# Shift and scale weights by single feature tiles, gates by way of DRAM rows, three output tiles begun early

## The chip, the cores and the metric

The kernel runs on one core of a Trainium2 chip. The metric is the device time of one execution in microseconds (us), median of several runs. The engines named below are TensorE (PE; its weight loads are listed as PEld), VectorE (DVE), ScalarE (ACT), GpSimd (POOL) and SyncE (SP, which here only issues DMAs). DMAs are issued from SP, ACT and POOL.

## The reference, cut to what matters

One inference step of a two-layer trunk over 512 latent and 128 context tokens, model width 1024. Layer 0 is gated attention (16 query heads, 4 key/value heads of 64), layer 1 a gated linear recurrence of 8 heads in both directions. Each layer is modulated by shift, scale and gate vectors that come from two conditioning vectors:

```python
def _adaln(cond, w, b):
    mod = jax.nn.silu(cond.astype(jnp.float32)) @ w.astype(jnp.float32) + b.astype(jnp.float32)
    return jnp.split(mod.astype(cond.dtype), 3, axis=-1)

for i in range(DEPTH):
    sh_p, sc_p, g_p = _adaln(c_ctx, ada_w[i], ada_b[i])
    sh_s, sc_s, g_s = _adaln(c, ada_w[i], ada_b[i])
    hp = xp * (1.0 + sc_p) + sh_p
    hs = xs * (1.0 + sc_s) + sh_s
    ...
    xp = _layer_norm(DEEPNORM_ALPHA * xp + g_p * out_p, ln_gain[i], ln_bias[i])
    xs = _layer_norm(DEEPNORM_ALPHA * xs + g_s * out_s, ln_gain[i], ln_bias[i])
```

The shift and the scale of layer 0 are needed before the first projection; a gate vector is needed only at the end of its layer, where it multiplies the rows of the output projection before the residual sum and the layer norm.

## The kernel before

Tokens stand in five tiles of 128 (four latent, one context). Feature-major operands have eight feature tiles (`ft`) of 128. Every product of weights and activations is three matmuls (high by high, high by low, low by high): a float32 weight piece of 128 x 1024 (512 KB, tile `raw`) is split by an ACT cast (line 218) and a DVE subtraction (line 219) into a high and a low part. `order` lists all pieces in the sequence in which SP loads them; `pump` issues the next loads while no more than a set number are ahead (8 at the start, then 2). Loads passed to `pin` keep their program order on SP. The program as written is not the order of the instructions: a planner places each engine's stream by program order and by when it reckons that inputs and buffers are ready, and for everything up to line 1037 it does so with a simulated timeline.

**The lead** (lines 415 to 483). Four rounds `c4`, each for two feature tiles. `flip` transposes x on TensorE. `ada_mms` multiplies SiLU(cond) by a piece of `ada_w` holding 256 columns and half of the depth, so a column chunk takes two pieces, and shift and scale take two chunks, four pieces, a round. `ada_row` copies the result out of PSUM, `ada_out` turns it into columns with two small matmuls (line 275) and adds the bias into `shsc` (line 279). `modulate` applies shift and scale on DVE (line 441) and splits into `hhi` (ACT, line 443) and `hlo` (DVE, line 444). `kv_mms` (lines 460 to 462) then accumulates keys and values of all five token tiles over the feature tiles. The rotary table and the two gains are loaded from POOL's queue at the start (lines 419, 421), and POOL makes four tables of them (line 424).

**The other modulation chunks** run beside attention. `q_gen` projects the queries of the next group as side work and calls `next(fill)` at fixed places, where `fill` is `ada_gen` over some chunks: the gate of layer 0 beside group 1, the shift, scale and gate of layer 1 later. For a gate chunk `ada_out` fills the column tile `gcol`, and `spread` (lines 285 to 292) broadcasts the columns over partitions: four matmuls against the identity (eight records, line 291, `gateps`) and a DVE copy into `gate` (line 292). For layer 0 that comes in `ada_gen`; for layer 1 in the tail.

**The second half.** `proj_gen(h)` projects head h of the recurrence (`vgps`, then three parts i = 0 to 2 in `rps`, lines 1108 to 1110), `evac` evaluates the gates of part i. `gla_gen(h)` runs the recurrence of a head beside the projection of the next head: seven levels (`lv`, line 1238 or 1244, with DVE updates of `A` at lines 1247 and 1252 and an ACT copy `kc` at line 1216), then `kp` (1278), `sp` (1284) with state updates on DVE (1287, 1290), `op` (1301 to 1304), a normalisation (1309 to 1315), `oT` (1320) and the split result `ghi`, `glo` (1321, 1322). `Residual` prepares the residual rows in DRAM on POOL. PSUM holds four tiles of two banks in this half.

**The tail** (lines 1368 to 1424). The last head's recurrence has no projection beside it. `weave` runs it with `tail_gen` at a ratio of 2.2 side steps per step: `tail_gen` splits the eight pieces of `rec_w_out` in the order `OUT1`, spreads the gate of layer 1, and accumulates k = 0 to 6 of the output tiles 0 and 1 (`out_mms`, lines 993 to 995, `outp`; k is the head). After the last head, k = 7 of these two and all of tiles 2, 3 and 4 follow, and `Norm` does gate, residual and layer norm of each tile on DVE (`half`: lines 1013 to 1015; `finish`: 1020 to 1030), one POOL power (line 189), and two output DMAs (line 1031).

Of the kernel before, what the change touches and what calls it, by code (L numbers as in the profile page):

```python
# [18 lines left out]
P = 128  # L19
# [112 lines left out]
def hybrid_step(ctx: ExitStack, tc: tile.TileContext, a: dict, o: dict):  # L132
# [49 lines left out]
    gcol1 = const.tile([P, 4, 2, 2], F32, name="gcol1")  # L182
# [12 lines left out]
    def pump():  # L195
        while order:
            start = order[0] in FIRST
            if len(ahead) >= (RAW_START if start else RAW_AHEAD):
                break
            src = order.popleft()  # L200
            if src[0] == "x":
                c = slice(src[1] * CW, (src[1] + 1) * CW)
                pin(nc.sync.dma_start(xt[:, :TS, c], a["xs"][:, c].rearrange("(t p) d -> p t d", p=P)))
                pin(nc.sync.dma_start(xt[:, TS, c], a["xp"][:, c]))
                continue
            raw = (raw0 if start else rawp).tile([P, 1024], F32, tag="raw", name="raw")
            (pass_on if src[0][:3] == "rec" else pin)(nc.sync.dma_start(raw, piece(src)))
            ahead.append((src, raw))
# [55 lines left out]

    def ada_row(ps):
        row = rowp.tile([P, CW], F32, tag="row", name="row")
        nc.vector.tensor_copy(row, ps[:, :CW])
        return row

    def ada_out(layer, c, row):  # L270
# [7 lines left out]
        if part < 2:  # L278
            nc.vector.tensor_tensor(shsc[layer][:, part, 2 * c4:2 * c4 + 2, :], src, bias, ALU.add)
            return None  # L280
        gcol = gcol1[:, c4] if layer else tiny.tile([P, 2, 2], F32, tag="gc", name="gcol")[:]
        nc.vector.tensor_tensor(gcol, src, bias, ALU.add)
        return None if layer else lambda: spread(layer, c4, gcol)

    def spread(layer, c4, gcol):

        ps = bank1("gateps")
        for s in range(2):
            for j in range(2):
                col = bass.AP(gcol.tensor, gcol.offset + 2 * j + s, [list(gcol.ap[0]), [0, P]])  # L290
                nc.tensor.matmul(ps[:, (2 * s + j) * P:(2 * s + j + 1) * P], col, ident, start=True, stop=True)
        nc.vector.tensor_copy(gate[layer][:, :, c4 * CW:(c4 + 1) * CW], ps[:].rearrange("p (a b) -> p a b", a=2))

    def ada_gen(chunks):
        todo, last = None, None
        for l, c in chunks:
# [3 lines left out]
            if last:  # L300
                last()
            last = todo and ada_out(*todo)
            yield
            todo = (l, c, ada_row(ps))
        if last:
            last()
        if todo:
            last = ada_out(*todo)
            yield
            if last:  # L310
                last()
                yield
# [21 lines left out]
    x1d = [dram.tile([P, D], F32, name=f"x1d{tt}") for tt in range(TT)]  # L334
    x1a = [dram.tile([P, D], F32, name=f"x1a{tt}") for tt in range(TT)]
# [27 lines left out]
    order.extend(("rec_w_out", nh, i) for nh, i in OUT1)  # L363
# [51 lines left out]
    with pool("xin", 1) as xin:  # L415
# [3 lines left out]
        nc.gpsimd.dma_start(rope, a["rope"])  # L419
        for g, nm in ((qg, "q_gain"), (kg, "k_gain")):  # L420
            nc.gpsimd.dma_start(g, a[nm].to_broadcast((P, HD)))
        nc.gpsimd.tensor_scalar(qg, qg, 1.0 / math.sqrt(HD), 1.0, ALU.mult, ALU.mult)
        for t, r, g in ((cosq, 0, qg), (sinq, 1, qg), (cosk, 0, kg), (sink, 1, kg)):
            nc.gpsimd.tensor_tensor(t, rope[:, r], view(g, 0, [[0, TS], [1, HD]]), ALU.mult)
# [39 lines left out]
        for c4 in range(4):  # L464
            if c4:
                kv_mms(2 * c4 - 2)
            flip(c4)
            rows = []
            for part in range(2):
                ps = bank1("adaps")  # L470
                for i in range(2):
                    ada_mms(ps, 0, 4 * part + c4, i)
                rows.append(ada_row(ps))
            if c4:
                kv_mms(2 * c4 - 1)
            for part in range(2):
                ada_out(0, 4 * part + c4, rows[part])
            modulate(2 * c4)
            modulate(2 * c4 + 1)
            kv_split(c4)  # L480
        first_w = Weights("attn_w_in", 0, LEAD_LO)
        kv_mms(6)
        kv_mms(7)
# [490 lines left out]
    side.finish()  # L974
    modA, modB = h1_mod()
# [13 lines left out]
    def out_mms(ps, tt, nh, ghi, glo, ks=range(KT)):  # L989
        t = slice(tt * P, (tt + 1) * P)  # L990
        for k in ks:
            hi, lo = wo[nh, k // 2]
            nc.tensor.matmul(ps[:, nh, :], ghi[:, k, t], hi[:, k % 2, :], start=(k == 0), stop=False)  # L993
            nc.tensor.matmul(ps[:, nh, :], ghi[:, k, t], lo[:, k % 2, :], start=False, stop=False)  # L994
            nc.tensor.matmul(ps[:, nh, :], glo[:, k, t], hi[:, k % 2, :], start=False, stop=(k == KT - 1))  # L995

    class Norm:
        def __init__(self, layer, tt, ps=None):
            self.layer, self.tt = layer, tt
            self.ps = bank2("outp") if ps is None else ps  # L1000
# [8 lines left out]
        def half(self, nh):  # L1009
# [3 lines left out]
            nc.vector.tensor_tensor(y, self.ps[:, nh, :], g, ALU.mult)  # L1013
# [49 lines left out]
    def proj_gen(h, H, first):  # L1063
# [292 lines left out]

    residual = Residual()
# [10 lines left out]
    outs = {}  # L1368

    def tail_gen():  # L1370

        gate[1] = g2.tile([P, 2, D], F32, tag="A", name="gate1")
        w1 = gsp.tile([P, 2, 1024], F32R, tag="gate", name="w1")
        slots = [w1[:, i, :] for i in range(2)]
        for _ in range(2):
            slots += [wr.tile([P, 1024], F32R, tag=t, name=t)[:] for t in ("whi", "wlo")]
        for tt in range(2):
            outs[tt] = bank2("outp")
        for n, (nh, i) in enumerate(OUT1):
            if n == 3:  # L1380
                w2 = gsp.tile([P, 5, 1024], F32R, tag="gs", name="w2")
                w3 = h1p.tile([P, 5, 1024], F32R, tag="h1lo", name="w3")
                slots += [t[:, i, :] for t in (w2, w3) for i in range(5)]
            hi, lo = slots[2 * n], slots[2 * n + 1]
            wo[nh, i] = tuple(t.rearrange("p (k n) -> p k n", k=2) for t in (hi, lo))
            split_piece(hi, lo, ("rec_w_out", nh, i), nc.vector)
            yield
            if nh == 0:
                continue
            spread(1, i, gcol1[:, i])  # L1390
            yield
            for tt in range(2):
                for k in (2 * i, 2 * i + 1)[:2 if i < 3 else 1]:
                    for nh in range(2):
                        out_mms(outs[tt], tt, nh, ghi, glo, [k])
                    yield

# [9 lines left out]
    side = Side(("t", tail_gen()))  # L1407
    weave(lane.gens[0][0], side, SIDE_T)
    side.finish()
# [7 lines left out]
    for tt in range(TT):  # L1417
        norm = Norm(1, tt, outs.get(tt))
# [40 lines left out]
def _layout(inputs):  # L1459
# [5 lines left out]
    r["small"] = np.concatenate([r["small"], cond, ada_b], axis=1)  # L1465
    r["ada_w0"], r["ada_w1"] = _chunks(g["ada_w"][0]), _chunks(g["ada_w"][1])
# [34 lines left out]
```

## Time and profile before

| | |
|---|---|
| Median of 3 runs | 887.74 us (887.34 to 892.66) |
| Profiled execution, own time | 883.77 us |
| Span in the profile | 881.9 us |
| Mean granted TensorE clock | 0.988 |

The page of the profile has the busy time of each engine, a chain of waits followed back from the last instruction, and groups of instructions by line. A row of the timeline reads: start in us, duration in us, engine, line, operation, output<-inputs, shape, count, and in brackets the engine's idle time before it and what ended that. A row of the table of windows reads: stretch, its length, busy time of PE, PEld, DVE, ACT and POOL with the count of instructions, the granted clock, the mean busy share of the 16 DMA engines, and GB/s; made for one line alone, it has only the engines that this line uses. A matmul's record is longer than the distance to the next, since they are pipelined. A float32 matmul has two records.

### The profile page before, as it was taken

What the parts mean: (1) busy time and instruction counts of PE and PEld (TensorE: products, weight loads), DVE (VectorE), ACT (ScalarE), POOL (GpSimd) and SP (SyncE); (2) the same over time, 40 slices, a digit from 0 to 9 for tenths busy, and PEclk for the clock granted to TensorE, in tenths of its full rate; (3) what the DMA queues carried; (4) which work ended last, traced back from release to release, by engine and by line L of the source; (5) the groups of instructions that cost most, each with busy time, mean ns of one, the idle gap of its engine ahead of it and who ended that gap; (6) DMA issues with size and microseconds to landing.
All of it is one profiled execution on the core that took longest, in us unless ns stands there. A gap on an engine that the chain in (4) does not pass through costs nothing.

```text
span 881.9 us, 19250 instructions
## 1 busy us (share of the span) xinstructions
PE 837.9 (95%) x8116; PEld 744.0 (84%) x8116; DVE 538.7 (61%) x972; ACT 374.1 (42%) x735; POOL 203.1 (23%) x250
## 2 busy tenths in 40 slices
PE   5999999989999998999999999999999999989995
PEld 3689998878878766788899999999999999987783
DVE  2456534664645657576437486676767585758495
ACT  2133536534554767422343453544434444444200
POOL 2013001422323733010000223243333224110110
PEclk9999999999999999999999999999999999998998
DMA  9922122143141136441131323231322323132121
GB/s 312 371 88 84 49 71 74 49 144 97 49 145 49 49 122 213 145 142 72 37 117 50 109 73 97 64 123 51 103 85 85 97 70 102 53 113 100 55 96 71
DMA packets 32678, 89.86 MB, mean 102 GB/s; under 512 B 4400, under 2 KB 11568, under 8 KB 32592
## 3 DMA queue, kind: packets, MB, share of 16 engines
q1 hardware_dynamic: 21984, 71.57, 24.6%
q0 software_dynamic: 3984, 12.13, 5.0%
q10 hardware_dynamic: 6624, 4.93, 1.8%
q8 instruction: 64, 1.05, 0.5%
q14 instruction: 22, 0.18, 0.1%
HBM read 79.44 MB, written 9.18 MB: 100 GB/s over the span
## 4 chain that ended last, share of the span: by engine, by line
PE 86%; DVE 4%; DMA 4%; ACT 2%; issue 1%; POOL 0%; SPq 0%; DVEq 0%; ACTq 0%; POOLq 0%
PE rps L1108 7%; PE rps L1109 6%; PE rps L1110 6%; PE vgps L1098 5%; PE vgps L1099 4%; PE vgps L1100 4%; PE outp L993 4%; PE outp L994 4%; PE outp L995 4%; PE pot L750 4%; PE pt L832 3%; PE adaps L261 2%; PE lv L1238 2%; PE gps L317 2%; PE gps L318 2%; PE gps L319 2%
## 5 line engine op out<-in xcount | busy, mean ns | idle before, releaser
L1108 PE MATMUL rps<-h1hi,rhi 128*128 128x320 f32 x368 | 118.2, 321 | 0.0
L1109 PE MATMUL rps<-h1lo,rhi 128*128 128x320 f32 x368 | 115.0, 312 | 0.0
L1110 PE MATMUL rps<-h1hi,rlo 128*128 128x320 f32 x368 | 113.9, 310 | 0.0
L825 POOL TENSOR_SCALAR p<-p,rc 128x640 f32<-128x640 f32 x64 | 53.4, 838 | 79.3 <-DVE rc L824 77.5
L1108 PEld LDWEIGHTS rps<-h1hi,rhi 128*128 128x128 f32 x368 | 69.8, 190 | 1.3
L1109 PEld LDWEIGHTS rps<-h1lo,rhi 128*128 128x128 f32 x368 | 69.3, 188 | 0.0
L1110 PEld LDWEIGHTS rps<-h1hi,rlo 128*128 128x128 f32 x368 | 69.3, 188 | 0.0
L219 DVE TENSOR_TENSOR rlo<-raw,rhi 128x1024 fp32r<-128x1024 f32 x32 | 46.0, 1441 | 34.3 <-ACT rhi L218 34.3
L820 ACT ACTIVATE p<-sc,nm 128x640 f32<-128x640 f32 x64 | 51.0, 799 | 30.9 <-DVE nm L817 23.2
L817 DVE TENSOR_REDUCE nm<-sc 128x1 f32<-128x640 f32 x64 | 52.1, 818 | 17.1 <-PE sc L724 16.7
L1266 POOL COPY At<-near 32x160 f32<-32x160 f32 x32 | 14.0, 438 | 198.1 <-DVE near L1228 197.1
L1216 ACT COPY kc<-A 128x640 f32<-128x640 f32 x40 | 32.1, 804 | 57.4 <-DVE A L1247 50.3
L218 ACT CAST rhi<-raw 128x1024 fp32r<-128x1024 f32 x32 | 33.5, 1048 | 50.5 <-PE rps L1109 47.6
L1098 PE MATMUL vgps<-rhi,h1hi 128*128 128x256 f32 x180 | 51.5, 286 | 1.2 <-ACT h1hi L948 1.2
L832 PE MATMUL pt<-small,p 128*128 128x128 f32 x320 | 49.1, 278 | 2.6 <-ACT pts L728 0.8
L1100 PE MATMUL vgps<-rhi,h1lo 128*128 128x256 f32 x180 | 50.9, 283 | 0.4 <-DVE h1lo L949 0.4
L1099 PE MATMUL vgps<-rlo,h1hi 128*128 128x256 f32 x180 | 50.9, 283 | 0.0
L728 ACT COPY pts<-pt 128x512 f32<-128x512 f32 x64 | 36.4, 586 | 28.2 <-PE pt L832 27.4
L723 PE MATMUL sc<-kk,X 128*128 128x320 f32 x128 | 43.0, 345 | 3.8 <-ACT p L820 3.3
L832 PEld LDWEIGHTS pt<-small,p 128*128 128x128 f32 x320 | 37.5, 143 | 8.2 <-issue 5.5
L1098 PE MATMUL vgps<-wspare,h1hi 128*128 128x256 f32 x140 | 41.7, 298 | 0.0
L317 PE MATMUL gps<-hhi,whi 128*128 128x320 f32 x128 | 40.0, 313 | 0.4 <-ACT X L576 0.4
(263 smaller groups left out, 2401.4 us busy)
## 6 DMA issues: line engine op xcount, KB each, us to landing
raw<-in_ada_w SPq DMA_DIRECT2D x48, 512.0 KB, 4.8
raw<-in_rec_w_in SPq DMA_DIRECT2D x40, 512.0 KB, 3.7
raw<-in_attn_w_in SPq DMA_DIRECT2D x16, 512.0 KB, 4.5
raw<-in_attn_w_out SPq DMA_DIRECT2D x8, 512.0 KB, 4.5
raw<-in_rec_w_out SPq DMA_DIRECT2D x8, 512.0 KB, 3.6
x1d<-y SPq DMA_DIRECT2D x5, 512.0 KB, 2.6
rx<-x1d POOLq DMA_DIRECT2D x20, 128.0 KB, 3.8
x1a<-rx POOLq DMA_DIRECT2D x20, 128.0 KB, 2.8
```

The source lines that it names most:

```text
L219: (lo_eng or nc.gpsimd).tensor_tensor(lo, raw, hi.bitcast(F32), ALU.subtract)
L317: nc.tensor.matmul(ps[:, :320], w.hi(k)[:, c], hhi[:, k, t], start=(k == 0), stop=False)
L817: nc.vector.tensor_reduce(nm[:, 0:1], sc[:, :, :320], AX.XY, ALU.max, negate=True)
L820: nc.scalar.activation(halves(p[:]), sc[:, :, :320], AF.Exp, bias=nm[:, 0:1], accum_out=su[:, 0:1])
L825: nc.gpsimd.tensor_scalar(p, p, rs[:, 0:1], 1.0, ALU.mult, ALU.mult)
L832: nc.tensor.transpose(pt[:, i * 256 + q * P:i * 256 + (q + 1) * P], ps[q][:, (k0 + i) * P:(k0 + i + 1) * P], ident)
L1098: nc.tensor.matmul(out, h1hi[:, k, t], hi, start=(k == 0), stop=False)
L1099: nc.tensor.matmul(out, h1hi[:, k, t], lo, start=False, stop=False)
L1100: nc.tensor.matmul(out, h1lo[:, k, t], hi, start=False, stop=(k == KT - 1))
L1108: nc.tensor.matmul(ps[:, j, :320], hi[:, k, :], h1hi[:, k, t], start=(k == 0), stop=False)
L1109: nc.tensor.matmul(ps[:, j, :320], hi[:, k, :], h1lo[:, k, t], start=False, stop=False)
L1110: nc.tensor.matmul(ps[:, j, :320], lo[:, k, :], h1hi[:, k, t], start=False, stop=(k == KT - 1))
```

## The change

Three things are changed.

1. The shift and scale columns of layer 0 are also laid out as `ada_m`: 16 pieces of 128 x 1024 that each hold one feature tile (128 columns) at full depth, shift tiles first. The lead runs in eight rounds, one per feature tile, with two pieces each (`ada_feat`, `ada_feat_out`). In `order` a round pair is: x, the two pieces of its first tile, its key/value piece, the two pieces of its second tile. The rotary table and the gains move from POOL's queue to a place in SP's order after the second pair; POOL makes the tables after the loop.
2. `spread` goes. `gcol` holds the whole gate as columns; `gate_rows` writes it as two rows into a DRAM tile, two DMAs on SP per layer, and `load_gate` reads each row back over 128 partitions: for layer 0 on SP after the queries of group 2, for layer 1 on POOL before the tail.
3. The tail's splits and fills are written out. The first `rec_w_out` piece is loaded before head 7's last `rec_w_in` piece; the first two pieces are split within head 7's third part; k = 0, 1 of the output tiles 0 and 1 come before and after its evaluation; a list `PLAN` gives what follows each step of the last recurrence, with a third output tile begun at `kp`. Tiles 3 and 4 use two half-used PSUM tiles each.

```diff
+    gcol = [const.tile([P, KT, 2], F32, name=f"gcol{i}") for i in range(2)]
...
+            if src[0] == "rope":
+                rope_loads()
+                continue
...
+    def ada_feat(ps, ft):
+        for part in range(2):
+            raw = take(("ada_m", part * KT + ft, 0))
+            for i in range(2):
+                for q in range(4):
+                    k = 4 * i + q
+                    nc.tensor.matmul(ps[32 * q:32 * q + 32, part * P:(part + 1) * P], sil[:, k, :], raw[:, k * P:(k + 1) * P],
+                                     start=(i == 0), stop=(i == 1))
+            pump()
+
+    def ada_feat_out(ft, row):
+        ps = bank1("adaps2")
+        for j in range(2):
+            nc.tensor.matmul(ps[:, 2 * j:2 * j + 2], row[:, j * P:(j + 1) * P], sel, start=True, stop=True)
+        nc.vector.tensor_tensor(shsc[0][:, :, ft, :], ps[:, :4].rearrange("p (a b) -> p a b", a=2),
+                                view(adab, ft, [[KT, 2], [0, 2]]), ALU.add)
...
-    def spread(layer, c4, gcol):
...
+    def gate_rows(layer):
+        for s in range(2):
+            nc.sync.dma_start(gated[layer][s].rearrange("(k p) -> p k", p=P), gcol[layer][:, :, s])
+
+    def load_gate(layer, queue):
+        for s in range(2):
+            queue.dma_start(gate[layer][:, s, :], gated[layer][s:s + 1, :].to_broadcast((P, D)))
...
     for c4 in range(4):
+        lead = [("ada_m", part * KT + 2 * c4, 0) for part in range(2)]
         order.append(("x", c4))
-        order.extend(ada_pieces([(0, 4 * part + c4) for part in range(2)]))
+        order.extend(lead)
         order.append(("attn_kv", 0, c4))
+        order.extend(("ada_m", part * KT + 2 * c4 + 1, 0) for part in range(2))
+        if c4 == 1:
+            order.append(("rope",))
...
-    order.extend(("rec_w_out", nh, i) for nh, i in OUT1)
+    order.insert(len(order) - 1, ("rec_w_out", *OUT1[0]))
+    order.extend(("rec_w_out", nh, i) for nh, i in OUT1[1:])
...
+        for ft in range(KT):
+            if ft % 2 == 0:
+                flip(ft // 2)
+            ps = bank1("adaps")
+            ada_feat(ps, ft)
+            row = ada_row(ps)
+            if ft % 2 == 0:
+                kv_split(ft // 2)
+            if ft:
+                kv_mms(ft - 1)
+            ada_feat_out(ft, row)
+            modulate(ft)
...
+        if c == 1:
+            gate_rows(0)
+        elif c == 2:
+            load_gate(0, nc.sync)
...
     side.finish()
+    gate_rows(1)
...
+        last = h == RH - 1
         for i in range(3):
+            if last and i == 2:
+                tail.split()
             if i:
                 load_q(i)
             yield from mms(i, 0)
+            if last and i == 2:
+                tail.split()
             yield from mms(i, 1)
+            if last and i == 2:
+                tail.fill(0, 0, (0, 1))
+                tail.fill(1, 0, (0, 1))
             evac(i)
...
+        def fill(self, tt, nh, ks):
+            if tt not in self.outs:
+                ps = bank2("outp")
+                self.outs[tt] = [ps[:, 0, :], ps[:, 1, :]]
+            out_mms(self.outs[tt], tt, nh, ghi, glo, ks)
...
+    PLAN = (["s"], [(0, 2), "s"], [(1, 2), "s"], [(0, 3), (1, 3), "s"], [(0, 4), "s"], [(1, 4), (0, 5)], [(1, 5)],
+            [(0, 6), (1, 6)], [(2, 0)], [(2, 1), (2, 2)], [(2, 3), (2, 4), (2, 5), (2, 6)])
...
-    side = Side(("t", tail_gen()))
-    weave(lane.gens[0][0], side, SIDE_T)
-    side.finish()
+    load_gate(1, nc.gpsimd)
+    for tt in range(2):
+        tail.fill(tt, 1, (0, 1))
+    tail.split()
+    last = lane.gens[0][0]
+    for jobs in PLAN:
+        next(last)
+        for job in jobs:
+            if job == "s":
+                tail.split()
+            else:
+                tt, k = job
+                for nh in range(2):
+                    tail.fill(tt, nh, (k,))
+    drain(last)
...
-        norm = Norm(1, tt, outs.get(tt))
+        norm = Norm(1, tt, outs.get(tt) or [bank2("outp")[:, 0, :] for _ in range(2)])
...
+    r["ada_m"] = _chunks(g["ada_w"][0][:, :2 * D], P)
```

More of the change, by code (lines that the diff above doesn't have):

```diff
@@ L279, in ada_out @@
             nc.vector.tensor_tensor(shsc[layer][:, part, 2 * c4:2 * c4 + 2, :], src, bias, ALU.add)
[L280 to L283, printed above, removed]
-    def spread(layer, c4, gcol):
-        ps = bank1("gateps")
+            return
+        nc.vector.tensor_tensor(gcol[layer][:, 2 * c4:2 * c4 + 2, :], src, bias, ALU.add)
+    def gate_rows(layer):
         for s in range(2):
[L289 to L292, printed above, removed]
+            nc.sync.dma_start(gated[layer][s].rearrange("(k p) -> p k", p=P), gcol[layer][:, :, s])
+    def load_gate(layer, queue):
+        for s in range(2):
+            queue.dma_start(gate[layer][:, s, :], gated[layer][s:s + 1, :].to_broadcast((P, D)))
     def ada_gen(chunks):
-        todo, last = None, None
+        todo = None
         for l, c in chunks:
@@ L334, in hybrid_step @@
     x1d = [dram.tile([P, D], F32, name=f"x1d{tt}") for tt in range(TT)]
+    gated = [dram.tile([2, D], F32, name=f"gated{i}") for i in range(2)]
     x1a = [dram.tile([P, D], F32, name=f"x1a{tt}") for tt in range(TT)]
@@ L418, in hybrid_step, with rope_loads @@
         rope = xin.tile([P, 2, TS, HD], F32, name="rope")
[L419 to L424, printed above, removed]
+        def rope_loads():
+            pin(nc.sync.dma_start(rope, a["rope"]))
+            for g, nm in ((qg, "q_gain"), (kg, "k_gain")):
+                pin(nc.sync.dma_start(g, a[nm].to_broadcast((P, HD))))
         h32 = xin.tile([P, KT, NT], F32, name="h32")
@@ L462, in kv_mms @@
                 nc.tensor.matmul(acc[tt], hlo[:, ft, t], hi, start=False, stop=(ft == KT - 1))
[L464 to L480, printed above, removed]
+        for ft in range(KT):
[10 more added lines that the diff above has]
+            modulate(ft)
+        nc.gpsimd.tensor_scalar(qg, qg, 1.0 / math.sqrt(HD), 1.0, ALU.mult, ALU.mult)
+        for t, r, g in ((cosq, 0, qg), (sinq, 1, qg), (cosk, 0, kg), (sink, 1, kg)):
+            nc.gpsimd.tensor_tensor(t, rope[:, r], view(g, 0, [[0, TS], [1, HD]]), ALU.mult)
         first_w = Weights("attn_w_in", 0, LEAD_LO)
-        kv_mms(6)
-        kv_mms(7)
+        kv_mms(KT - 1)
     r0.close()
@@ L999, in __init__ @@
             self.layer, self.tt = layer, tt
-            self.ps = bank2("outp") if ps is None else ps
+            ps = bank2("outp") if ps is None else ps
+            self.ps = [ps[:, 0, :], ps[:, 1, :]] if not isinstance(ps, list) else ps
             if layer == 0:
@@ L1406, in hybrid_step @@
         load_resid(tt)
-    side = Side(("t", tail_gen()))
-    weave(lane.gens[0][0], side, SIDE_T)
-    side.finish()
+    gate[1] = g2.tile([P, 2, D], F32, tag="A", name="gate1")
+    load_gate(1, nc.gpsimd)
[13 more added lines that the diff above has]
+    drain(last)
+    outs = tail.outs
     gx.close()
```

68 lines of the change are left out of this document (27 added, 41 removed).

## The prediction

> **What bounds the kernel now.** I read the page first (busy time, chain of waits), then a table of windows by stage, then the timeline of the stages that the change touches.
>
> ```profile
> span 881.9 us, 19250 instructions
> PE 837.9 (95%) x8116; PEld 744.0 (84%) x8116; DVE 538.7 (61%) x972; ACT 374.1 (42%) x735; POOL 203.1 (23%) x250
> PE 86%; DVE 4%; DMA 4%; ACT 2%; issue 1%; POOL 0%; SPq 0%; DVEq 0%; ACTq 0%; POOLq 0%
> core 0: us, PE busy (x) PEld busy (x) DVE busy (x) ACT busy (x) POOL busy (x), PEclk, DMA share, GB/s
> 0.00:21.10 21.10, 10.81 (x60) 6.64 (x61) 5.57 (x16) 3.90 (x6) 5.25 (x13) 1.00 0.92 309
> 24.30:66.00 41.70, 40.78 (x285) 30.80 (x284) 20.86 (x40) 10.93 (x14) 2.75 (x2) 1.00 0.62 222
> 185.00:201.00 16.00, 13.78 (x101) 11.10 (x99) 6.97 (x15) 5.21 (x8) 2.22 (x3) 0.81 0.39 132
> 350.00:789.55 439.55, 436.25 (x4960) 410.19 (x4956) 281.24 (x451) 186.07 (x356) 98.41 (x137) 1.00 0.29 87
> 789.55:795.16 5.61, 0.74 (x6) 0.53 (x6) 5.54 (x8) 5.54 (x8) 1.21 (x3) 0.74 0.83 280
> 795.16:799.30 4.14, 4.14 (x53) 3.74 (x54) 3.46 (x4) 2.70 (x4) 0.00 (x0) 0.52 0.68 238
> 799.30:818.80 19.50, 19.18 (x332) 14.81 (x331) 17.04 (x29) 6.39 (x12) 2.26 (x4) 1.00 0.12 34
> 836.60:872.20 35.60, 34.31 (x146) 26.84 (x144) 28.45 (x51) 0.00 (x0) 5.07 (x6) 1.00 0.25 89
> 872.20:881.90 9.70, 0.00 (x0) 0.00 (x0) 5.12 (x9) 0.00 (x0) 0.95 (x1) 0.60 0.14 54
> ```
>
> TensorE carries the chain (86%) and is never more than a few per cent idle from 24 us to 789 us, so work taken off it in the middle is worth up to its own length. The reader should see four places where it is not the bound: the first 21.1 us (10.3 us idle, DMA share 0.92); 185 to 201 us (2.2 us idle and a granted clock of 0.81); the gap before the last head's recurrence (4.9 of 5.6 us idle, then clock 0.52); and the last 9.7 us, DVE and output DMAs alone.
>
> The sum is made against the profiled execution, 883.77 us (span 881.9 and 1.9 around it). The median of the runs is 887.74, 4.0 us (0.45%) above it; I subtract the same gain from the median.
>
> **Part 1: the lead by single feature tiles.** Before, `modulate` of the first tile waits for four `ada_w` pieces (two column chunks, shift and scale); after, for two `ada_m` pieces. Rope and the two gains go from POOL's queue to SP's, behind the pieces of c4=1.
>
> ```profile
> 5.06 2.37 PE L434 MATMUL xps<-small,xt 128*128 128x128 f32 x10 [5.06 <-DMA xt<-in_xs]
> 12.11 1.08 PE L261 MATMUL adaps<-raw,sil 128*32 128x256 f32 x8 [1.11 <-DMA raw<-in_ada_w]
> 13.26 0.42 DVE L267 COPY row<-adaps 128x256 f32<-128x256 f32 x1 [5.37 <-PE adaps L261]
> 14.49 1.02 PE L275 MATMUL adaps<-small,row 128*128 128x2 f32 x4
> 19.44 1.51 DVE L441 TENSOR_SCALAR h<-h,shsc 128x512 f32<-128x512 f32 x4
> 20.32 0.72 ACT L443 CAST hhi<-h 128x640 fp32r<-128x640 f32 x1 [3.27 <-DVE h L441]
> 21.10 0.80 PE L460 MATMUL acc<-kvhi,hhi 128*128 128x512 f32 x1 [0.79 <-ACT hhi L443]
> 45.00 1.29 PE L434 MATMUL xps<-small,xt 128*128 128x128 f32 x10
> 46.75 1.07 PE L261 MATMUL adaps<-raw,sil 128*32 128x256 f32 x16 [0.46 <-ACT h L436]
> ```
>
> The second piece landed at 12.1. Without 320 KB of rope and gains in front (1.0 us at 309 GB/s) I put it at 11.1, then 1.08 (matmuls) + 0.42 (row) + 1.02 (turn) + 0.16 (shsc, an estimate from its 4 columns) + half of 1.51 + 0.72 and some 0.5 of handovers: the first `kv_mms` at 15.8, 5.3 us earlier. But TensorE did useful work in 10.8 of the first 21.1 us; by 15.8 it will have done one flip, two pieces and one turn (2.4 + 2.2 + 1.0 = 5.6). The other 5.2 us move behind the start, 2.6 if they then run at full clock. That leaves 0 to 2.7, say 1.4. The count of matmul columns, rows and turns is the same (16 pieces of 8 matmuls of 128 columns for 16 of 4 of 256); the doubled weight loads I cost at nothing, since PEld is busy 6.6 us where PE is 10.8, and without that cover they fall inside the upper end below.
>
> Against it stands a new wait. There are eight rounds instead of four, and in each the chain from `shsc` to `kv_mms` must be covered: 0.16 + 0.75 + 0.73 + handovers = 2.0 us. A round that begins with a flip has flip and pieces (1.29 + 1.07) to cover it; the other four have 1.07, so up to 0.9 us each is bare, unless the first query matmuls fill it as they do now.
>
> I take 1.4 gained less one bare stretch, **-0.5** us, for the lead. Ends: -5.3 (whole head start kept) and +3.6 (four bare rounds, no head start). SP's three added DMAs sit behind pieces loaded eight ahead; the rope tables are built on POOL, idle in that stretch (2.75 busy of 41.7 us).
>
> **Part 2: gates by DRAM rows.** `spread` goes: per layer four times 8 matmul records and a DVE copy.
>
> ```profile
> 170.00:201.00 31.00, 6.13 (x32) 5.29 (x32) 0.90 0.31 103
> 193.78 0.61 PE L275 MATMUL adaps<-small,row 128*128 128x2 f32 x4 [0.83 <-DVE row L267]
> 197.66 2.08 PE L291 MATMUL gateps<-small,gcol 128*128 128x128 f32 x8 [0.54 <-DVE gcol L282]
> 199.39 0.81 PE L574 MATMUL qps<-identr,qs 128*128 128x128 f32 x4
> 191.49 43.27 SPq L207 DMA_DIRECT2D raw<-in_ada_w  x8
> 332.37 31.78 SPq L207 DMA_DIRECT2D raw<-in_attn_w_out  x8
> ```
>
> The first row is the table of windows for L291 alone (PE, PEld, clock, DMA share, GB/s): 6.1 us of TensorE for layer 0, of which the last spread takes 2.08 with TensorE waiting for it and at a low clock. Without them the query transposes (199.39) wait only for the row that 193.78 waited for and a short DVE and ACT chain (0.4 + 0.4 + 0.4 + 0.4 with handovers, about 195.6): 3.8 less, and 1.0 for the first spread, less what the stage takes back elsewhere. I take **-4**; ends 0 (DVE and ACT chains set the stage anyway) and -6.1. Layer 1's four spreads count in part 3. `ada_gen` yields one step less, which I cost at nothing.
>
> Added on SP: two row DMAs per layer with 1024 four-byte runs each, and two broadcasts of 512 KB for layer 0. Behind them in SP's queue stand the `ada_w` and `attn_w_out` pieces, used at 43.27/8 = 5.4 us and 31.78/8 = 4.0 us apiece with two held ahead: 10.8 and 8 us of cover.
>
> ```profile
> q1 hardware_dynamic: 21984, 71.57, 24.6%
> q10 hardware_dynamic: 6624, 4.93, 1.8%
> ngain<-in_norm_gain ACTq DMA_DIRECT2D x1, 0.5 KB, 2.8
> ```
>
> No row has 1024 tiny runs. Share times 16 engines times 881.9, by packets: 38 ns per packet on q10 (0.7 KB mean), 158 on q1 (3.3 KB). 1024/16 = 64 per engine: 2.4 us or 10.1 us per DMA, on top of the 2.8 that 128 four-byte runs took to land. I take 2.4, since q10 is the nearer in size: 4.9 us a layer, inside the cover, cost 0. At 10.1 (20.2 a layer) it overruns: rival C.
>
> The Trainium skill, DMA: Bandwidth & Descriptors, section Measured (HBM→SBUF, 128 partitions, SWDGE, issued from GpSimd), gives about 10.5 ns per packet for a small DMA, and its Specifications say that under 512 B an engine reads, modifies and writes. As an estimate by that page a row DMA takes 10.8 us and a layer 21.5, 10.7 and 13.5 beyond the cover, so that the sum would be 900.2. No run here shows it.
>
> **Part 3: the tail.** `Tail` splits the first `rec_w_out` pieces inside head 7's projection, fills k=0,1 of two tiles where TensorE stands idle at 789.55, and does k=0 to 6 of a third tile between the last head's kp, sp, op and oT.
>
> ```profile
> 797.50 1.04 ACT L218 CAST w<-raw 128x1024 fp32r<-128x1024 f32 x1 [1.44 <-DMA raw<-in_rec_w_out]
> 818.79 1.04 PE L1278 MATMUL kp<-small,A 128*128 128x128 f32 x8
> 820.93 2.05 PE L1284 MATMUL sp<-v,kt 128*128 128x128 f32 x16
> 824.90 0.38 PE L1301 MATMUL op<-v,At 128*128 128x128 f32 x2
> 833.27 0.74 PE L1320 MATMUL oT<-small,on 128*128 128x128 f32 x5 [1.61 <-DVE on L1315]
> 836.60 1.29 DVE L1013 TENSOR_TENSOR y<-outp,gate 128x512 f32<-128x512 f32 x2 [0.84 <-PE outp L995]
> L1013 DVE TENSOR_TENSOR y<-outp,gate 128x512 f32<-128x512 f32 x10 | 6.7, 681 | 7.8 <-PE outp L995 7.8
> 800.20 0.69 DVE L292 COPY gate<-gateps 128x512 f32<-128x512 f32 x1
> 814.72 2.38 POOL L1266 COPY At<-near 32x160 f32<-32x160 f32 x4 [23.96 <-DVE near L1228]
> ```
>
> After 836.6 less is left: three k=7 parts and two whole tiles, 18 + 96 matmuls at 34.31/146 = 0.23 are 26 us instead of 35.6. DVE needs 28.45 + 5.12 = 33.6 us for its five tiles, so it becomes the bound. The row of L1013 in the groups by line, DVE only and from 836.6 on, says what that is worth: it waited 7.8 us for TensorE in all, and that goes. **-7.8**.
>
> Before that point the recurrence's own chain sets the pace, not TensorE (DVE 17.0 of 19.5 us busy). The idle 4.9 us get filled, but the first level still waits for ACT and DVE, both busy 5.54 of 5.61; warming the clock buys nothing on that chain. Two of the four gate copies, 0.69 each, leave DVE between 795 and 819: **-1.4**. The third tile's fills (6, 12 and 24 matmuls at 0.23) go into what is bare between kp, sp, op and oT, which stand 2.1, 4.0 and 8.4 apart with 1.0, 2.1 and some 2.8 of matmuls of their own: 1.4 into 1.1, 2.8 into 1.9, 5.5 into 5.6: **+1**. The gate's two broadcasts (1 MB) join the three residual loads that POOL issues in the gap's window, just when an ACT cast already waits 1.44 us for its piece at the head of ACT's queue: **+1**; ends 0 and +3 (1 MB at the 280 GB/s of that window is 3.7). POOL's own next work comes at 814.7, and the gate is first read at 836.6, so nothing else waits for them.
>
> The first `rec_w_out` piece is loaded ahead of head 7's last `rec_w_in` piece, which so lands one load later (512 KB, 1.7 us at 309 GB/s); the 48 matmuls of the part before it cover that, and uncovered it would cost 1.7.
>
> Tail: -7.8 - 1.4 + 1 + 1 = -7.2; ends -9 and -3. **Sum: -0.5 - 4 - 7.2 = -11.7.** 883.8 becomes 872.1 in a profile like this one, and the median 887.74 becomes 876.0.
>
> **Rivals.** A, all of it lands: lead -5.3, attention -6.1, tail -9, in all -20.4: 867.3. For it: TensorE is 95% busy. Against: eight bare chains and an ACT and DVE bound recurrence.
> B, the gain is given back: the instructions of the first half are ordered anew, the lead loses 2.6, attention gains only 2, the casts block the tail (+3 instead of +1, no credit for the copies: -3.8): -3.2, 884.5. For it: the stall at 797 us is a load that came late, and that stays. Against: DVE's 7.8 us of waiting needs only TensorE to be early.
> C, slower: the row DMAs hold SP's rings. At 158 ns a packet a layer's two take 20.2 us, 9.4 and 12.2 beyond the cover of 10.8 and 8: 876.0 + 21.6 = 897.6. It decides once a layer's rows take over about 15 us, when the loss (twice that less 18.8) eats the 11.7. For it: no row with so many tiny runs. Against: 128 of them landed in 2.8 us.
>
> **How the numbers follow.** My forecast 0.50, its own range 870 to 882; A 0.14, B 0.26, C 0.10. A difference under 1% (8.9 us) cannot be told from no change here, so faster means under 878.9: A and four fifths of my case, 0.55. Slower: C and a little of B, 0.11. Same: 0.34. The range runs from just below A, 866, to beyond B, 887; it leaves out C and a little of A.
>
> **What would show it.** Lead: the first L460 row near 16 us instead of 21.1, and idle before `acc` in odd rounds under 0.9. Attention: no gateps rows, and the qps row of 199.39 some 4 to 5 us nearer the adaps before it; a row DMA landing within about 5 us. Tail: no idle stretch over 1 us before the first lv, PEclk 1.00 there, and L1013 with almost no wait for outp after the last head. It would be wrong if the first lv slipped by more than 2 us, if DVE still waited 5 us or more for outp, or if TensorE waited for `raw` behind a row DMA.

## The result, and the profile after

| | before | after |
|---|---|---|
| Median | 887.88 us (7 runs, 887.34 to 892.66) | 894.47 us (7 runs, 891.40 to 899.70) |
| Profiled execution, span | 883.77, 881.9 | 895.32, 893.5 |

The ratio is 1.0067 (95% interval 1.0043 to 1.0091): 6.0 us slower, where the prediction said 876.0 and a range of 866 to 887. A few marks of the two traces, each the start of the same operation, show where:

| Mark | before | after | difference |
|---|---|---|---|
| first key/value matmul | 21.10 | 12.82 | -8.3 |
| two sums into `gs` early in attention (DVE) | 162.49, 177.09 | 157.56, 172.15 | -4.9 |
| fifth last sum into `gs` | 327.46 | 337.33 | +9.9 |
| last sum into `gs` | 361.37 | 380.57 | +19.2 |
| `kp` of the last head | 818.79 | 837.58 | +18.8 |
| end of the span | 881.9 | 893.5 | +11.6 |

So the lead gained 4.9 us, attention lost 24.1, and the tail gained 7.2. These are marks of two single executions that lie 11.6 us apart where the medians lie 6.6 apart, so that some 5 us of the differences come with the executions profiled; the prices further down are taken from the ratios in the table of runs. The page of the profile after (busy time of each engine, and the shares of the chain of waits) shows DMA with 6% of the chain where it had 4%:

```profile
PE 831.6 (93%) x8180; PEld 743.9 (83%) x8180; DVE 534.2 (60%) x964; ACT 373.4 (42%) x735; POOL 201.4 (23%) x249
PE 85%; DMA 6%; DVE 4%; ACT 2%; issue 1%; POOL 0%; DVEq 0%; ACTq 0%
```

The table of windows of the profile after, in the columns explained above: the two stalls in attention, then the lead, then the tail (projection's end to the first `lv`, to `kp`, to the first gate product, to the end).

```profile
185.00:208.00 23.00, 7.92 (x57) 5.62 (x55) 5.07 (x12) 4.80 (x14) 1.82 (x2) 0.63 0.56 78
345.00:370.00 25.00, 20.04 (x123) 15.61 (x118) 12.16 (x24) 13.16 (x24) 4.93 (x7) 0.73 0.75 145
0.00:12.82 12.82, 5.56 (x62) 4.11 (x62) 3.90 (x11) 3.86 (x5) 0.42 (x5) 1.00 0.84 301
12.82:60.10 47.28, 44.74 (x405) 36.78 (x406) 25.43 (x49) 12.53 (x16) 5.76 (x7) 0.96 0.75 278
808.37:814.51 6.14, 6.14 (x31) 4.82 (x29) 6.07 (x8) 6.09 (x8) 1.34 (x3) 1.00 1.00 382
814.51:837.58 23.07, 19.35 (x361) 14.74 (x361) 18.89 (x31) 8.36 (x15) 2.26 (x4) 1.00 0.19 69
837.58:856.11 18.53, 17.65 (x104) 15.28 (x105) 4.93 (x12) 3.65 (x14) 1.20 (x1) 1.00 0.22 64
856.11:893.50 37.39, 24.63 (x108) 19.82 (x106) 32.55 (x60) 0.00 (x0) 6.03 (x7) 0.87 0.27 99
```

In 185 to 208 us TensorE is idle for 15.1 us, no engine is busy for more than 8, and the DMA engines are busy for 0.56 of the time while they move 78 GB/s: many small packets (of the 3119 of 180 to 215 us, 2192 are under 512 B). What happens there, in SP's timeline:

```profile
174.40 7.88 SPq L210 DMA_DIRECT2D raw<-in_attn_w_in  x2
189.06 1.01 SPq L307 DMA_DIRECT2D gated<-gcol  x2
190.16 1.48 SPq L210 DMA_DIRECT2D raw<-in_ada_w  x3
199.58 3.63 SPq L311 DMA_DIRECT2D gate<-gated  x2
207.68 34.23 SPq L210 DMA_DIRECT2D raw<-in_ada_w  x5
```

and in the table of DMA issues of 180 to 215 us (the last number is the median time from issue to landing):

```profile
raw<-in_ada_w SPq DMA_DIRECT2D x5, 512.0 KB, 16.3
gate<-gated SPq DMA_DIRECT2D x2, 512.0 KB, 9.7
gated<-gcol SPq DMA_DIRECT2D x2, 4.0 KB, 11.9
```

The two row DMAs, 4 KB each, take 11.9 us; the `ada_w` pieces issued right behind them land after 16.3 us instead of some 4.3, and TensorE's timeline shows who waits:

```profile
190.00 0.50 PE L590 MATMUL qps<-identr,qs 128*128 128x128 f32 x4 [1.24 <-DVE qs L583]
206.55 1.08 PE L264 MATMUL adaps<-raw,sil 128*32 128x256 f32 x8 [12.23 <-DMA raw<-in_ada_w]
```

The second stall is of another kind. In ACT's timeline a cast of an `attn_w_out` piece waits 5.30 us, and with it the exponentials queued behind it on ACT, for which TensorE then stands 4.4 us; that piece was issued at 351.1, 1.4 us *ahead* of layer 1's row DMAs (352.6), and took 10.0 us:

```profile
353.52 1.06 ACT L221 CAST wohi<-raw 128x1024 fp32r<-128x1024 f32 x1
361.14 1.04 ACT L221 CAST wohi<-raw 128x1024 fp32r<-128x1024 f32 x1 [5.30 <-DMA raw<-in_attn_w_out]
```

SP's own waits, in the table of waits of its queue, give the rival explanation: in SP's order the rows stand ahead of the pieces, and SP stood for the column, then for the landed rows.

```profile
SPq L307 <- DVE gcol L302: 6.7, 1, 6.7
SPq L311 <- DMA gated<-gcol: 8.4, 2, 7.9
```

### The profile page after: what moved, and what is told of

Read it like the earlier page. It is cut to its first block, busy times and chain, and to the rows that moved or that the text cites. A ratio compares the mean times of both kernels' runs of the same rounds, so it can differ in the third digit from the quotient of the medians.

```text
span 893.5 us, 19387 instructions
## 1 busy us (share of the span) xinstructions
PE 831.6 (93%) x8180; PEld 743.9 (83%) x8180; DVE 534.2 (60%) x964; ACT 373.4 (42%) x735; POOL 201.4 (23%) x249
## 4 chain that ended last, share of the span: by engine, by line
PE 85%; DMA 6%; DVE 4%; ACT 2%; issue 1%; POOL 0%; DVEq 0%; ACTq 0%
PE rps L1130 7%; PE rps L1131 6%; PE rps L1132 6%; PE vgps L1120 5%; PE vgps L1122 4%; PE vgps L1121 4%; PE outp L1014 4%; PE pot L766 4%; PE outp L1016 4%; PE outp L1015 4%; PE pt L848 3%; DMA raw<-in_ada_w 2%; PE lv L1268 2%; PE gps L330 2%; PE gps L331 2%; PE gps L332 2%
## 5 line engine op out<-in xcount | busy, mean ns | idle before, releaser
L848 PE MATMUL pt<-small,p 128*128 128x128 f32 x320 | 51.8, 288 | 2.8 <-ACT pts L744 1.3
L739 PE MATMUL sc<-kk,X 128*128 128x320 f32 x128 | 45.1, 361 | 7.6 <-ACT p L836 7.1
L848 PEld LDWEIGHTS pt<-small,p 128*128 128x128 f32 x320 | 39.6, 149 | 9.2 <-issue 4.7
L766 PE MATMUL pot<-pts,vv 128*64 128x256 f32 x320 | 40.5, 390 | 0.5 <-DVE pts L744 0.5
```

Of the source, the lines that this page charges most:

```text
L766: nc.tensor.matmul(pot[j * HD:(j + 1) * HD, :CW], vv[:, slot, c * HD:(c + 1) * HD], moving[j], start=first, stop=last)
L848: nc.tensor.transpose(pt[:, i * 256 + q * P:i * 256 + (q + 1) * P], ps[q][:, (k0 + i) * P:(k0 + i + 1) * P], ident)
```

## The experiments

Three theories of the loss in attention: R, the four-byte runs of the row DMAs hold the DMA rings, so that loads near them land late; Q, SP's queue waits for the column and for the rows, and holds the loads back whatever their shape; P, the planner's new order of the first half costs by itself. All results, each beside runs of the kernel before on the same chip (1% is 8.9 us):

| Run | Median us (runs) | Ratio to before (95%) |
|---|---|---|
| after | 894.47 (7) | 1.0067 (1.0043 to 1.0091) |
| wide | 880.62 (7) | 0.9906 (0.9878 to 0.9935) |
| before_rows | 899.16 (4) | 1.0126 (1.0076 to 1.0176) |
| before_few | 887.96 (10) | 1.0022 (0.9998 to 1.0045) |
| before_quiet | 888.14 (1) | one run, no interval |
| rows_act | 878.20 (4) | 0.9881 (0.9823 to 0.9940) |
| wide_off | 877.54 (10) | 0.9889 (0.9861 to 0.9918) |
| wide_act | 874.50 (6) | 0.9866 (0.9831 to 0.9901) |
| wide0_act | 877.04 (6) | 0.9876 (0.9838 to 0.9914) |
| wide1_act | 884.43 (12) | 0.9962 (0.9939 to 0.9985) |
| lead_only | 883.88 (10) | 0.9947 (0.9925 to 0.9970) |
| gates_only | 887.94 (10) | 1.0004 (0.9981 to 1.0027) |
| no_tail | 882.67 (12) | 0.9944 (0.9924 to 0.9965) |
| wide_off_two | 883.24 (12) | 0.9982 (0.9960 to 1.0003) |

### The shape of the rows, against SP's wait and the planner

**wide**: the same rows in 16 runs of 512 B. `gcol` is laid out as `[P, 2, KT]` (that hunk is left out here), and

```diff
 def gate_rows(layer):
-    for s in range(2):
-        nc.sync.dma_start(gated[layer][s].rearrange("(k p) -> p k", p=P), gcol[layer][:, :, s])
+    ps = bank1("gateps")
+    cols = gcol[layer][:].rearrange("p s k -> p (s k)")
+    nc.tensor.matmul(ps[:2 * KT, :P], cols, ident, start=True, stop=True)
+    grow = rowp.tile([P, P], F32, tag="grow", name="grow")
+    nc.vector.tensor_copy(grow[:2 * KT], ps[:2 * KT, :P])
+    nc.sync.dma_start(gated[layer][:].rearrange("s (k p) -> (s k) p", p=P), grow[:2 * KT])
```

> The changed kernel, with the gate rows of a layer written as 16 runs of 512 B (gcol turned by one matmul, one copy, one DMA) in place of 2048 runs of four bytes. Theory R (the small runs of the row DMAs hold the DMA rings, and the weight pieces beside and behind them land late): the attention's loss of 24 us goes, 870 to 876 us, no adaps wait for raw over 4 us, rows land within 4 us. Theory Q (SP's queue, which waits for gcol and then for gated, holds the loads back, whatever the shape): the waits are still there and longer by a matmul and a copy, 892 to 898. Theory P (the planner's new order of the first half is what costs): also 890 to 898.

Measured 880.62: 1.6% (14.3 us) below the changed kernel, so P falls and R has most of the loss; but it is 5 us above what R alone forecast. The row DMA landed in 1.4 us, and the first `adaps` matmul behind it waited 1.45 us for its piece instead of 12.23 (table of DMA issues, TensorE's timeline).

```profile
gated<-grow SPq DMA_DIRECT2D x1, 8.0 KB, 1.4
```

```profile
194.71 1.08 PE L264 MATMUL adaps<-raw,sil 128*32 128x256 f32 x8 [1.45 <-DMA raw<-in_ada_w]
```

**before_rows**: the kernel before, plus the row DMAs at the same places. The hunks that keep both layers' columns in `gcols` and make the DRAM tile are left out here.

```diff
+    def extra_rows(layer):
+        for s in range(2):
+            nc.sync.dma_start(rows_d[layer][s].rearrange("(k p) -> p k", p=P), view(gcols[layer], s, [[2, KT]]))
...
     def q_next(c):
         yield from q_gen(c, Xs[c], ada_gen(ADA_B[c - 1]))
+        if c == 1:
+            extra_rows(0)
...
     side.finish()
+    extra_rows(1)
```

> The kernel before with nothing taken out, and only the row DMAs added at the same places (after the second query chunk's loads, and between the attn_w_out pieces), to DRAM that nobody reads. Theory R: 15 to 28 us slower than before (903 to 916), with one stall on raw near 195 us and one on attn_w_out near 345 us. Theory P: within 3 us of before (885 to 891). Theory Q: 5 to 8 us slower (the 6.7 us that SP waits for gcol), and none of it where the column is ready.

Measured +11 us (7 to 16), below R's 15 to 28 and above Q's 5 to 8; P falls again. The stall is the one of the changed kernel, in the table of DMA issues (190 to 215 us) and in TensorE's timeline:

```profile
raw<-in_ada_w SPq DMA_DIRECT2D x4, 512.0 KB, 15.0
rowsd<-gcol SPq DMA_DIRECT2D x2, 4.0 KB, 11.2
```

```profile
212.94 1.08 PE L262 MATMUL adaps<-raw,sil 128*32 128x256 f32 x8 [10.89 <-DMA raw<-in_ada_w]
```

**before_few** writes the same 8 KB from the same places, in one DMA a layer of 128 runs of 64 B (the edit against before_rows):

```diff
-        for s in range(2):
-            nc.sync.dma_start(rows_d[layer][s].rearrange("(k p) -> p k", p=P), view(gcols[layer], s, [[2, KT]]))
+        nc.sync.dma_start(rows_d[layer][:].rearrange("s (p k) -> (s p) k", k=2 * KT), gcols[layer][:].rearrange("p a b c -> p (a b c)"))
```

> The run before_rows with the same 8 KB in 128 runs of 64 B, one DMA a layer, at the same places of SP's queue. Theory R (the number of runs is what costs) with Q (SP's wait for the column costs some 4 us beside it): 3 to 5 us slower than before, 891 to 894, rows land within 3 us. If the place and the wait are all: as before_rows, 897 to 901. If the wait costs nothing either: 886 to 890.

Measured +2.0 us (-0.2 to 4.0). Place and wait are those of before_rows; only the form of the rows differs (128 runs of 64 B in one DMA for 2048 of four bytes in two), and 9.2 us (1.04%) go: that is R. That the number counts, and not the length alone, is borne out by a load of before, 128 four-byte runs, which landed in 2.8 us (`ngain` in the prediction). What the wait costs without the four-byte runs lies between nothing and 4 us. Time from issue to landing of the two DMAs:

```profile
DMA to landing us min/median/max: 1.4/2.4/3.4
```

**before_quiet** issues the four-byte rows of both layers from `shsc`, which is ready early (the edit against before_rows):

```diff
-            nc.sync.dma_start(rows_d[layer][s].rearrange("(k p) -> p k", p=P), view(gcols[layer], s, [[2, KT]]))
+            nc.sync.dma_start(rows_d[layer][s].rearrange("(k p) -> p k", p=P), shsc[0][:, layer, :, s])
```

> The kernel before, with the two four-byte row DMAs of a layer issued near 105 us, where the DMA share is 0.2 and no load is late, from columns that are long ready, to DRAM that nobody reads. Theory R: each lands only after 9 to 12 us, even alone, and the time stays within 3 us of before because pieces are loaded 8 us apart there. Rival (rows are slow only because pieces share the rings): they land in 3 to 5 us.

The planner put them at 57.3 us, not at 105, all four together with the `attn_w_in` pieces behind them. They took 11.5 to 13.9 us each, and the time did not move beyond the spread of before (888.14, runs of before beside it 882.54 to 892.08). So the rows are slow also where no load is in flight ahead of them, though four at once, and not one alone as was meant. The loads behind them were late too (one `attn_w_in` piece took 22.0 us), but TensorE stood for none of them: rows are harmless where nothing in their reach is wanted soon. Table of DMA issues, 30 to 125 us:

```profile
rowsd<-shsc SPq DMA_DIRECT2D x4, 4.0 KB, 12.7
```

**rows_act** sends the four-byte rows of the changed kernel from ACT.

```diff
-            nc.sync.dma_start(gated[layer][s].rearrange("(k p) -> p k", p=P), gcol[layer][:, :, s])
+            nc.scalar.dma_start(gated[layer][s].rearrange("(k p) -> p k", p=P), gcol[layer][:, :, s])
```

> The changed kernel with the same four-byte rows issued by ACT instead of SP. Theory R in its narrow form (only what stands behind them in SP's own ring is held): the loss goes, 870 to 878. Theory R in its wide form (the 16 engines are held for every ring): 885 to 895, pieces still land in 10 us or more. Theory Q: SP no longer waits for gcol, 6 to 8 us come back, 886 to 889.

Measured 878.20 (873.12 to 883.36): the loss goes although the runs are as small as before. The time is that of R's narrow form; the trace speaks against it. The rows, sent by ACT at 190.4, take until about 201, when the gate loads that wait for them go out. The three `ada_w` pieces that SP issued ahead of them landed in 4.7 us; the two that SP issued from 193 on, while ACT's rows were in flight, took 12.6 and 13.0. Tables of DMA issues of 186 to 190.3 and of 193 to 200 us:

```profile
raw<-in_ada_w SPq DMA_DIRECT2D x3, 512.0 KB, 4.7
```

```profile
raw<-in_ada_w SPq DMA_DIRECT2D x2, 512.0 KB, 12.8
```

Layer 1 shows the same: behind ACT's rows of 337.6, two `attn_w_out` pieces on SP took 13.5 and 12.6 us. So loads are held from whichever queue the rows come, as in R's wide form. The loss went because of the order: SP no longer waited for the column, `ada_w` went out at 186.78 instead of 190.16, ahead of the rows, and was there when TensorE wanted it at 191.98; the two held pieces were wanted only from 205 us on, and TensorE did not stand for them. This run changes the queue and SP's wait at once; before_few, which keeps the wait, is the one that parts R from Q.

### SP without waits

wide left SP standing: its timeline has no issue between the end of `attn_w_in` at 181.0 and the row DMA, and the next `ada_w` pieces came behind that.

```profile
173.46 7.56 SPq L210 DMA_DIRECT2D raw<-in_attn_w_in  x2
190.11 0.34 SPq L312 DMA_DIRECT2D gated<-grow  x1
190.55 1.32 SPq L210 DMA_DIRECT2D raw<-in_ada_w  x3
```

**wide_off** is wide with `nc.scalar.dma_start` for the row DMA and `load_gate(0, nc.gpsimd)`; **wide_act** has the first of these two alone.

> The run wide, with the row DMA issued by ACT and the two broadcasts of layer 0's gate by POOL, so that SP carries nothing but weight pieces. Theory Q for the rest (in wide SP stood from 181 to 190 us waiting for the turned column, and the next ada_w piece came 4 us late): 4 us below wide, 874 to 878 us, and the ada_w issue after 182 us moves to 187 or earlier. Rival (the rest is the planner's order, or pieces that come late anyway): 879 to 882.

> The run wide with its one row DMA issued by ACT; layer 0's two broadcasts stay on SP. Theory Q for what wide still lost (SP stood 9 us for the turned column): 874 to 878. Rival (no such cost): as wide, 879 to 882.

wide_off came to 877.54 and wide_act to 874.50: in theory Q's range both, but the intervals of the ratios overlap with that of wide (by 0.4%, 3.6 us, wide_act is the lower). The mechanism is plain in wide_act's timeline, where the pieces go out 4.0 us earlier:

```profile
186.53 2.47 SPq L210 DMA_DIRECT2D raw<-in_ada_w  x3
```

wide_off is not better than wide_act: with the gate loads on POOL it is POOL that stands for the landed row (9.3 us in the trace of wide_off_two below, which loads the gate in the same way), with its other work behind that. wide_act is the fastest kernel of the study: 11.9 us (8.8 to 15) below before.

### The layers apart

**wide0_act** and **wide1_act** are wide_act with the four-byte rows on SP kept for layer 1 or for layer 0 alone.

```diff
 def gate_rows(layer):
+    if layer == 0:
...
+        return
     for s in range(2):
```

(the turned form for layer 0; wide1_act has it for layer 1).

> The run wide_act with layer 1's rows as four-byte runs on SP again, between the attn_w_out pieces, as in the changed kernel. Theory R: the second stall of the changed kernel's trace comes back, 8 to 10 us above wide_act, a wohi cast waits 4 us or more for its piece, and the first output matmul comes 6 to 9 us later after the last query group. Rival (the whole loss came from layer 0): within 2 us of wide_act.

> The changed kernel with layer 1's rows turned and sent by ACT, layer 0's four-byte rows left on SP as they are. If layer 0's rows with SP's two waits are the whole loss: as the changed kernel, 892 to 897 us, and the second stall (last query groups) stays without any row beside it. If layer 1's rows cost their part where the pieces slipped behind the first stall: 6 to 7 us less, 886 to 889, and no wohi cast waits over 4 us.

Layer 1's rows alone cost 0.1% (0.9 us, within the interval): my theory of a second stall failed there. Layer 0's alone cost 0.96% (8.5 us). Both together cost 2.01% (17.8 us), so layer 1's rows cost 9.3 us *beside* layer 0's (some 6 to 12, by the intervals of the two ratios). The waits for pieces between 175 and 400 us show the first stall in wide1_act:

```profile
PE adaps L264 <- DMA raw<-in_ada_w: 11.7, 2, 10.3
ACT wohi L221 <- DMA raw<-in_attn_w_out: 5.4, 3, 3.9
```

The wait of the `wohi` casts in this table does not tell the cases apart: it is 5.2 us in before and 6.2 in wide_act, which have no four-byte rows, and its longest part falls behind attention. What counts is where it falls. In wide1_act the four casts within attention waited 0.8 us at most, so the second stall is gone.

In wide0_act, too, the second stall is missing: the four pieces that attention splits went out at 325.2 to 332.2, the rows at 332.7, and none of their four casts waited a microsecond; the last two:

```profile
334.49 1.05 ACT L221 CAST wohi<-raw 128x1024 fp32r<-128x1024 f32 x1 [0.22 <-DMA raw<-in_attn_w_out]
337.02 1.05 ACT L221 CAST wohi<-raw 128x1024 fp32r<-128x1024 f32 x1 [0.21 <-DMA raw<-in_attn_w_out]
```

In the changed kernel the fourth piece was still on its way. before_rows has the same stall: its fourth piece went out 0.8 us ahead of the rows and took 8.2 us, and its cast waited 3.88. Why such a piece took 10.0 us with the rows 1.4 us behind it, 8.2 with 0.8, and only 5.1 in wide0_act with 0.8, stays open.

### The three parts alone

**lead_only** is the kernel before with the hunks of part 1; **gates_only** is before with part 2 in the form of wide_act (rows turned and sent by ACT, layer 1's gate loaded by POOL at the head of `tail_gen`); **no_tail** has both, with the tail of before; **wide_off_two** is wide_off without the third tile's early part:

```diff
-            [(0, 6), (1, 6)], [(2, 0)], [(2, 1), (2, 2)], [(2, 3), (2, 4), (2, 5), (2, 6)])
+            [(0, 6), (1, 6)])
```

> The kernel before with part 1 alone (single feature tiles, rope on SP). The marks of the changed kernel's trace say -4.9 us by the first query group: 883 us. The prediction's term was -0.5: 887.4.

> The kernel before with part 2 alone, done without its cost: spread gone, rows turned on TensorE, 16 runs of 512 B on ACT. The prediction's terms: -4 in the attention and -1.4 for the gate copies, 0.994 of before or less. Rival (where the spreads stood TensorE waits for the next ada_w piece instead): 0.998 to 1.001 of before.

> The run wide_act with the tail of before (output tiles begun in tail_gen, two of them, gate loaded by POOL): parts 1 and 2 without part 3. The prediction's tail term without the gate copies: 5.8 to 7 us above wide_act. Rival (the earlier fills are worth nothing because the recurrence paces the tail): within 2 us of wide_act.

> The run wide_off without the third output tile's early part (its fills leave the plan, the tile is computed whole at its turn). Theory T (the tail gains because DVE never waits for outp; TensorE then has 156 matmuls of 0.23 us after the last head, 35.9 us against DVE's 33.6): DVE waits 2 to 4 us for outp again, 1.5 to 3.5 us slower than wide_off. Rival (two tiles begun early are enough): within 1 us of wide_off.

lead_only: -4.7 us (-2.7 to -6.7). gates_only: +0.4 us (-1.7 to 2.4), the rival's case. no_tail against wide_act: 0.78%, the tail is worth 6.9 us. wide_off_two against wide_off: 0.93%, 8.2 us, more than the 1.5 to 3.5 expected. DVE waited 5.0 us for `outp` where wide_act and the changed kernel have 1.3. TensorE, without the fills, stood 5.02 us ahead of `oT`, whose five matmuls then took 1.30 us (0.71 in wide_act, with the fills). From the first gate product on the stretch is 6.7 us longer, of which DVE's wait for `outp` is 3.7 and its busy time 1.5; the rest was not taken apart. Timeline and table of waits of wide_off_two, then windows after the first gate product in wide_off_two and in wide_act:

```profile
827.45 1.30 PE L1355 MATMUL oT<-small,on 128*128 128x128 f32 x5 [5.02 <-DVE on L1350]
```

```profile
DVE y L1040 <- PE outp L1021: 5.0, 4, 3.3
```

```profile
831.39:875.50 44.11, 34.35 (x150) 27.81 (x149) 34.06 (x60) 0.00 (x0) 5.87 (x7) 0.93 0.24 84
```

```profile
834.59:872.00 37.41, 24.64 (x108) 19.82 (x106) 32.55 (x60) 0.00 (x0) 6.03 (x7) 0.86 0.27 98
```

## Why the prediction was wrong, point by point

**The step that failed is the price of the row DMAs**: "I take 2.4, since q10 is the nearer in size: 4.9 us a layer, inside the cover, cost 0." A row DMA takes 10.1 to 13.9 us from issue to landing in before_rows and before_quiet. Packets of 0.7 KB were a bad neighbour for runs of four bytes; the other end of the bound, 10.1 us, was right for one, though by luck: it is the time of packets of 3.3 KB. For the two of a layer it was too much: they overlap, and in before_rows the second landed 12.7 us after the first was issued, not 20.2. The estimate by the Trainium skill (DMA: Bandwidth & Descriptors, section Measured), 10.8 us per row DMA and, doubled by the prediction, 21.5 a layer, fares likewise: the runs agree with the first and not with the second.

The cover failed too. "with two held ahead: 10.8 and 8 us of cover" came from a mean over a stage; at this place the raw buffers held `attn_w_in` pieces, so that even in rows_act the first piece wanted at 192.0 went out only at 186.8, 5.2 us before, and took 3.9 to land. With a cover near 1 us, layer 0's rows cost 8.5 us; rival C had 9.4. Layer 1's cost 9.3 beside them; C had 12.2. C, with a chance of 0.10, was the case that came, and its 21.6 is 17.8. That it came so near is in part luck: its 20.2 us a layer was some 7.5 too long and its cover nearly 10 too large. And the rows do not hold SP's rings alone: in rows_act they held SP's loads from ACT's queue. The prediction's own sign of being wrong, TensorE waiting for `raw` behind a row DMA, is the 12.23 us above.

**SP's wait** was not in the sum. I named the pieces behind the rows but not that SP would stand for `gcol` (6.7 us) and for the landed rows. Without four-byte rows it is worth 0 to 4 us by before_few and some 3.6 by wide against wide_act; neither excludes zero. With them it decides which pieces fall behind the rows: rows_act, which has the rows and not SP's wait for the column, is 1.86% (16.5 us) below the changed kernel. Layer 0's loss needs both.

**Attention, "I take -4"** (and "-1.4" for two copies): the local effect is there and the gain is not. In gates_only the query transposes that stood at 199.39 start at 194.40, 5.0 us earlier; what is late next is a piece: in its timeline `adaps` waits again at the end of attention. By time the whole of part 2 without its cost is worth -1.7 to +2.4 us. Where each microsecond was given back was not traced further; single traces of this stage differ by 1 to 3 us (from 327.46 to 344.14 in the trace of before, whose execution was 4 us under its median, 1.0 longer in before_few, 2.5 in before_quiet, 2.7 in lead_only).

```profile
194.40 0.70 PE L572 MATMUL qps<-identr,qs 128*128 128x128 f32 x4 [1.24 <-DVE qs L565]
334.12 0.88 PE L261 MATMUL adaps<-raw,sil 128*32 128x256 f32 x8 [1.88 <-DMA raw<-in_ada_w]
```

**Lead, -0.5 taken, -4.7 measured**: right in kind, wrong in size. The first `kv_mms` came at 12.82, not 15.8, since the second piece landed near 8.4 us (6.2 after its issue, where it took 9.8 in before) and not at 11.1. Up to the same mark in attention (windows of before and of after):

```profile
0.00:162.49 162.49, 149.83 (x1061) 130.53 (x1062) 80.26 (x161) 62.50 (x111) 25.80 (x29) 1.00 0.44 149
```

```profile
0.00:157.56 157.56, 146.31 (x1189) 132.56 (x1190) 80.80 (x160) 62.51 (x111) 24.13 (x26) 0.99 0.43 154
```

TensorE's idle time fell by 1.4 us (12.66 to 11.25), which is what I kept; the bare stretch that I took off is already in it. The other 3.5 us are busy time. Part of it is that less of the work is done at TensorE's slow pace of the first stretch, 10.2 us of busy time where it was 14.0: with matmuls of 512 columns 0.43 us apart there and 0.23 later, these 3.8 us are worth some 1.8. The rest was not traced. In the timeline after, five matmuls of 512 columns take 1.9 us until 17.5, and 1.3 from there on; in before that change comes at 24 us:

```profile
12.82 1.91 PE L479 MATMUL acc<-kvhi,hhi 128*128 128x512 f32 x5 [1.06 <-ACT hhi L462]
15.68 1.99 PE L480 MATMUL acc<-kvlo,hhi 128*128 128x512 f32 x5
17.51 1.30 PE L481 MATMUL acc<-kvhi,hlo 128*128 128x512 f32 x5
```

**Tail, -7.2 predicted, -7.2 in the trace, -6.9 by time**: right. From the first gate product to the end of the span it took 45.3 us and takes 37.4 (-7.9; -7.8 foretold). The table of waits for DVE in that stretch has 1.3 us for `outp`:

```profile
DVE y L1035 <- PE outp L1016: 1.3, 3, 0.8
```

The fills cost 0.7 between `kp` and that product (1 foretold), and the stretch from the projection's end to the first `lv` grew from 5.61 to 6.14 with the DMA share at 1.00 (1 foretold). From `lv` to `kp`, where the two gate copies were to give 1.4, the time fell by 0.6 (23.63 and 23.07). No idle time is left before the first `lv`, and the granted clock there is 1.00, as said.

By ratios the parts add up: -4.7 + 0.4 - 6.9 + 17.8 = 6.6, where 6.0 was measured. wide_act, which has the change without the cost of its rows, came to 874.50 where the prediction said 876.0; that the sum meets it is partly chance, since a lead four microseconds larger makes up for gates that gave nothing.

## What to carry to other kernels

Count the contiguous runs of a DMA, not its bytes: turn a column into rows on TensorE first (one matmul, one copy) when it must go to DRAM. Tiny runs sent from another queue still hold the loads in flight with them, so see that the loads wanted next are out before them, and that the queue of the loads does not stand for a computation. Price an operation that no row shows from both ends, and when the far end would eat the gain, give it the weight of an open question rather than choose the near end. A cover is read at the place itself (which buffers are free, when the next piece goes out), not from the mean spacing of a stage.

## What the runs showed of the hardware

- A DMA of 1024 runs of four bytes took 10.1 to 13.9 us (before_rows, before_quiet), 128 runs of 64 B took 1.4 to 3.4 (before_few), 16 runs of 512 B took 1.4 (wide). Four in flight together (before_quiet, 11.5 to 13.9 each) took little longer than two (before_rows, 10.1 to 12.2).
- 512 KB loads in flight with such a DMA land late, from whichever queue. Behind two of them on SP they took 15.0 us (before_rows) and 16.3 (after), where the median of `ada_w` loads in the changed kernel is 4.3; on SP with the rows on ACT 12.6 and 13.0 (rows_act). Pieces issued on SP shortly ahead of them took 10.0 (after), 8.2 (before_rows) and 5.1 (wide0_act).
- The first matmuls of this kernel run at about half pace (0.43 us apart at 512 columns, 0.23 later), while the granted clock in the table of windows reads 1.00 in the first 21.1 us of before and the first 12.8 of after. The Trainium skill (TensorE: Matmul & The Clock Gate, section What's actually happening) says that a half-rate clock is the default, and is released by a busy window of about 3.4 us. The durations agree with the half rate; the clock column of the profile shows it only in part (0.64 from 12.82 to 17.51 us of after), and no run here tests the length of the window.
